# Gate weights as half sums over 512 columns, four gate blocks open, and branch products two to a bank

## The chip, the core and the metric

The kernel is one program on one core of one Trainium2 chip. The time is the device time of one execution in microseconds. Three executions of the kernel before took 3128.62, 3154.54 and 3169.11 us, median 3154.54. A further execution was recorded by the profiler; it took 3130.84 us, and every row below is from it.

## What is computed

Two layers of a diffusion backbone over 256 latent tokens (stream x) and 256 context tokens (stream xc), 1024 channels, float32. Each layer has a token mixer with four branches (window attention, differential attention, a convolution, a pooling mixer) and then a feed-forward part that looks up 16 of 16384 experts for each of 8 heads and each token. The changed code is in the merge of the four branches:

```python
def merge_branches(h, ys, w_gate, b_gate, w_branch, w_out):
    acc = jax.nn.sigmoid(h @ w_gate[0] + b_gate[0]) * (ys[0] @ w_branch[0])
    for n in range(1, N_BRANCH):
        acc = acc + jax.nn.sigmoid(h @ w_gate[n] + b_gate[n]) * (ys[n] @ w_branch[n])
    return acc @ w_out
```

Here `h` is 256x1024 (tokens x channels), each `w_gate[n]` 1024x1024, each `ys[n]` 256x512 and each `w_branch[n]` 512x1024. The sums over 1024 and 512 channels are sums of products of 128 channels each on TensorE (PE).

The expert lookup reads, for each token and each chosen expert, one row of 1024 numbers of a table `u` and one of a table `v` from the chip's memory by index (gathers): 6 tiles of 128 tokens, 128 experts for each token, a `u` and a `v` row each.

## The kernel before, in words

**Stages.** The program runs in this order. (1) The mixer of the first layer for the context tokens (to about 410 us); its products are computed with float32 split into two parts (class `Split`), three matmuls for one. (2) The mixer of the first layer for the latent tokens (to about 1060 us), with the gathers of the first context tile in the background. (3) Gathers almost alone (to about 1760 us). (4) The mixer of the second layer, with the last context tile's gathers in the background (to about 2270 us). (5) The rest of the second layer, whose gathers end the program.

**The merge.** A branch's 1024 output channels are 8 blocks of 128. `both` works on four blocks at a time, called a quad below: it loads 512 columns of the branch's weights (tile `w`, 1 MB), then twice 256 columns of the gate's weights for all 1024 channels (tile `w`, 1 MB each). For each block, `gate_mm` sums 8 products of the gate in a PSUM bank, ScalarE (ACT) takes a tanh of it (L844, into `th`), `branch_mm` sums 4 products of the branch in another bank, and VectorE (DVE) multiplies and adds both into `accT` (L851 to L854). Both sums come from the two banks of tag `mm`. There are 8 quads in stage 1, 8 in stage 2 and 4 in stage 4; `gates`, the gate part alone, runs for two more branches in stage 4, where the tanh values are kept.

**Weights.** All weight tiles `w` are loaded by one queue (SP's, L228 in `wtile`) into three places of 1 MB:

```python
    def wplace(kb, c):
        return sb.tile([128, 2048], F, tag="w", name="w", bufs=WB)[:, :kb * c].rearrange("p (k c) -> p k c", k=kb)
```

with `WB = 3`. A load can be issued when the tile that last had its place has been read for the last time. SP issues in program order. The search for experts (`route`) takes the same places for its weights `w_q`, and the output projection (`out_proj`) for `w_out`. In stage 1, a loaded tile is copied into two parts (L173 on ACT, L174 on DVE), which live in row buffers `u` and `v`; then `w` itself is free again.

**Background.** `tick` puts pieces of other work (attention, convolution, pooling) between products of the merge, `pump` puts in gathers (`u_slot`, `v_slot`): a POOL instruction that starts a gather (L1018), a DVE instruction for each `u` row (L1026), and for each `v` row a DVE instruction (L1043) or two matmuls (L1050). The order of the instructions on each engine is fixed when the program is built, by a list scheduler that follows this order as a priority; on the chip each engine works through its list in order.

**PSUM.** Eight banks: two `mm`, two `at` (attention scores), two `tr` (transposes and attention outputs), and two for the gathers' sums `va`. The scheduler orders accesses of two engines to a bank, even where they touch different halves of it.

Of the kernel before, what the change touches and what calls it, by code (L numbers as in the profile page):

```python
# [8 lines left out]
F = mybir.dt.float32  # L9
# [5 lines left out]
OP = mybir.AluOpType  # L15
# [33 lines left out]
def body(ctx: ExitStack, tc: tile.TileContext, x_d, cc_d, cols_d, rows_d, w_mod, w_in, w_gate,  # L49
# [8 lines left out]
    def mm_ps():  # L58
        return pp.tile([128, 512], F, tag="mm", name="mm", bufs=2)
# [10 lines left out]
    def t2():  # L70
        return sb.tile([128, 512], F, tag="t2", name="t2", bufs=4)

# [782 lines left out]

    def gates(hT, N, l, n, dst_of):
        for c in range(4):
            w = wtile(w_gate[l, n, :, c * 256:(c + 1) * 256], like=hT)
            for b in range(2):
                gate_mm(w, b, hT, N, l, n, c * 2 + b, dst_of(c * 2 + b))  # L860

# [5 lines left out]

    def both(hT, ys, N, l, order, accT, first):

        for c in range(2):  # L870
            for n in order:
                wb = wtile(w_branch[l, n, :, c * 512:(c + 1) * 512], 4, 512, ys[n])
                for c2 in range(2):
                    w = wtile(w_gate[l, n, :, c * 512 + c2 * 256:c * 512 + (c2 + 1) * 256], like=hT)
                    for b in range(2):
                        blk = c * 4 + c2 * 2 + b
                        th = sb.tile([128, T], F, tag="th", name="th", bufs=2)
                        gate_mm(w, b, hT, N, l, n, blk, th)
                        branch_mm(wb, c2 * 2 + b, ys[n], N, th, accT[:, blk, :], first and n == order[0])

# [371 lines left out]
    ysplit(3, hk(4), kv_half("k", 0))  # L1252
    both(hc, ys, T, 0, (3,), accT, True)
    flush()
# [3 lines left out]
    pieces(cv, 16 - CV)  # L1258
    both(hc, ys, T, 0, (0,), accT, False)
    ysplit(1, ysb(0), hk(1)[:, 0])  # L1260
    both(hc, ys, T, 0, (1,), accT, False)
    flush()
    ysplit(2, ysb(1), kv_half("k", 0))
    both(hc, ys, T, 0, (2,), accT, False)
    while mods:
# [51 lines left out]
    credit[1] = RATE0[1]  # L1317
    both(h, ys, T, 0, (3,), accT, True)
# [3 lines left out]
    both(h, ys, T, 0, (0,), accT, False)  # L1322
    TICKS[1] = T2[2]
    credit[1] = RATE0[3]
    both(h, ys, T, 0, (1,), accT, False)
    flush()
    credit[1] = RATE0[4]
    both(h, ys, T, 0, (2,), accT, False)
    out_proj(accT, (2, 3), 0)
# [24 lines left out]
    accT = hslot()  # L1354
    both(h, ys, T, 1, (3,), accT, True)
    flush()
# [6 lines left out]
    TICKS[1] = T3  # L1363
    both(h, ys, T, 1, (2,), accT, False)
    tha = [ysb(2 + i) for i in range(2)]
    thc = [m4() for i in range(2)]
    gates(h, T, 1, 0, lambda blk: tha[blk // 4][:, blk % 4, :])
    gates(h, T, 1, 1, lambda blk: thc[blk // 4][:, blk % 4, :])

# [154 lines left out]
```

## Time and profile before

| what | us |
|---|---|
| executions shown | 3128.62, 3154.54, 3169.11 |
| profiled execution | 3130.84 |
| its span | 3129.0 |
| busy in it: PE, DVE, POOL, ACT | 2336.2, 2330.6, 1744.7, 667.8 |

The busy times are sums over stages that have different limits, and no engine is busy for more than three quarters of the span. A stage has to be read by itself: who waits in it, and for what. The time from a weight load's issue to its landing stands in the view of DMA issues, the wait that it causes in the view of waits, and the release of its place on SP's own timeline.

### The profile page before, as it was taken

Reading aid. Unit: us, or ns where it says so; the run is one execution under the profiler, and the core shown is the slowest. Engines: PE = TensorE matmul, PEld = TensorE weight load, DVE = VectorE, ACT = ScalarE, POOL = GpSimd, SP = SyncE. Lnnn points to the kernel's source line nnn. Section 1 sums busy time; section 2 is a strip of 40 time slices with the busy share of each in tenths; the row PEclk is TensorE's granted clock in tenths of the full one; section 3 lists DMA queues with packets and bytes.
Section 4 is the critical chain, followed back from the end, with each engine's and each line's share of the span. In section 5 each row is a group of like instructions: output and inputs, shape, how many; then the busy total and the mean of one; then the engine's idle time right before and its main releaser. Section 6 shows DMA issues by size and latency. Waiting matters only on the chain.

```text
span 3129.0 us, 32834 instructions
## 1 busy us (share of the span) xinstructions
PE 2336.2 (75%) x10524; PEld 1561.6 (50%) x10524; DVE 2330.6 (74%) x5221; ACT 667.8 (21%) x1577; POOL 1744.7 (56%) x1542
## 2 busy tenths in 40 slices
PE   7999998879876776665555589769997875545555
PEld 5878887667765542222111267557686542211111
DVE  5956669768987899957677759876657995566776
ACT  3445421223111221111000201023331221110001
POOL 0000027554355687777777757666404677777776
PEclk9999999989998897787688899889998998977888
DMA  9948978887799899999999999899947889999998
GB/s 309 318 140 262 312 248 312 306 295 280 284 348 359 326 386 380 337 365 359 389 409 406 353 332 387 313 362 338 347 162 261 277 313 388 408 341 395 403 409 332
DMA packets 436779, 1036.53 MB, mean 331 GB/s; under 512 B 30464, under 2 KB 226560, under 8 KB 436608
## 3 DMA queue, kind: packets, MB, share of 16 engines
q0 software_dynamic: 221184, 805.40, 68.0%
q1 hardware_dynamic: 211984, 226.25, 21.7%
q10 hardware_dynamic: 3440, 2.78, 0.3%
q8 instruction: 84, 1.38, 0.2%
q14 instruction: 87, 0.71, 0.1%
HBM read 1032.22 MB, written 2.10 MB: 331 GB/s over the span
## 4 chain that ended last, share of the span: by engine, by line
PE 28%; DVE 20%; issue 18%; DMA 17%; POOL 16%; ACT 1%; SPq 0%; ACTq 0%; POOLq 0%; DVEq 0%
PE mm L215 12%; POOL v L1018 10%; POOL u L1018 6%; DMA v<-in_v_dram,idx 5%; DVE u L1026 5%; DMA w<-in_w_gate_dram 4%; DMA u<-in_u_dram,idx 3%; DVE m L774 3%; DVE dacc L1043 2%; PE mm L213 2%; PE mm L211 2%; DMA w<-in_w_in_dram 2%; PE mm L212 2%; PE at L473 2%; PE va L1050 2%
## 5 line engine op out<-in xcount | busy, mean ns | idle before, releaser
L1018 POOL DMA_INDIRECT u<-in_u_dram,idx x768 | 859.9, 1120 | 933.9 <-DVE m L804 428.9
L1050 PE MATMUL va<-v,dg 128*128 128x512 f32 x1436 | 843.4, 725 | 533.1 <-DMA v<-in_v_dram,idx 450.6
L1026 DVE SCALAR_TENSOR_TENSOR u<-u,h 128x1024 f32<-128x1024 f32 x768 | 934.2, 1221 | 295.1 <-DMA u<-in_u_dram,idx 293.5
L1018 POOL DMA_INDIRECT v<-in_v_dram,idx x768 | 884.2, 1151 | 432.6 <-issue 182.9
L1050 PEld LDWEIGHTS va<-v,dg 128*128 128x128 f32 x1436 | 295.9, 222 | 1023.6 <-issue 789.8
L215 PE MATMUL mm<-hT,w 128*128 128x256 f32 (+1 forms) x2176 | 509.7, 385 | 114.3 <-DMA w<-in_w_gate_dram 79.3
L1043 DVE SCALAR_TENSOR_TENSOR dacc<-v,wt,dacc 128x1024 f32<-128x1024 f32 x403 | 516.3, 1281 | 94.8 <-DMA v<-in_v_dram,idx 80.7
L215 PEld LDWEIGHTS mm<-hT,w 128*128 128x128 f32 x2176 | 406.6, 203 | 189.3 <-issue 74.9
L1048 ACT ACTIVATE dg<-ident,wt 128x128 f32<-128x128 f32 x359 | 141.4, 400 | 933.0 <-PE va L1050 859.0
L774 DVE SCALAR_TENSOR_TENSOR m<-m,cols,m 128x256 f32<-128x256 f32 x360 | 158.9, 478 | 0.1
L212 PE MATMUL mm<-hT,whi 128*128 128x256 f32 x512 | 143.9, 281 | 0.8 <-DVE hT L174 0.8
L211 PE MATMUL mm<-hT,whi 128*128 128x256 f32 x448 | 128.1, 286 | 4.0 <-ACT whi L173 3.2
L213 PE MATMUL mm<-hT,whi 128*128 128x256 f32 x448 | 127.2, 284 | 1.2 <-DVE whi L174 0.8
L215 PE MATMUL mm<-w,hT 128*128 128x256 f32 x512 | 118.5, 391 | 5.9 <-DMA w<-in_w_in_dram 5.9
L174 DVE TENSOR_TENSOR whi<-w,whi 128x1024 fp32r<-128x1024 f32 x86 | 104.1, 1221 | 16.4 <-ACT whi L173 8.9
L215 PEld LDWEIGHTS mm<-w,hT 128*128 128x128 f32 x512 | 100.0, 197 | 22.0 <-issue 7.8
L173 ACT CAST whi<-w 128x1024 fp32r<-128x1024 f32 x86 | 88.4, 1048 | 66.9 <-PE mm L213 49.9
L215 PE MATMUL mm<-ys,w 128*128 128x256 f32 x384 | 95.0, 385 | 6.3 <-ACT th L844 3.9
L212 PEld LDWEIGHTS mm<-hT,whi 128*128 128x128 f32 x512 | 97.3, 190 | 1.7 <-DVE hT L174 1.0
L844 ACT ACTIVATE th<-mm,cols 128x256 f32<-128x256 f32 x80 | 37.9, 474 | 268.8 <-PE mm L215 217.4
L211 PEld LDWEIGHTS mm<-hT,whi 128*128 128x128 f32 x448 | 85.5, 191 | 6.4 <-ACT whi L173 3.9
L213 PEld LDWEIGHTS mm<-hT,whi 128*128 128x128 f32 x448 | 85.0, 190 | 6.8 <-DVE whi L174 3.6
(339 smaller groups left out, 2831.7 us busy)
## 6 DMA issues: line engine op xcount, KB each, us to landing
w<-in_w_gate_dram SPq DMA_DIRECT2D x48, 1024.0 KB, 11.7
w<-in_w_in_dram SPq DMA_DIRECT2D x42, 1024.0 KB, 10.6
X<-in_w_mod_dram SPq DMA_DIRECT2D x40, 512.0 KB, 5.3
wm<-in_w_mod_dram SPq DMA_DIRECT2D x40, 512.0 KB, 5.3
w<-in_w_branch_dram SPq DMA_DIRECT2D x20, 1024.0 KB, 8.0
w<-in_w_q_dram SPq DMA_DIRECT2D x20, 1024.0 KB, 15.5
u<-in_u_dram,idx POOLq DMA_INDIRECT x768, 6.5
v<-in_v_dram,idx POOLq DMA_INDIRECT x768, 6.6
```

What stands on the lines that cost most here:

```text
L173: nc.scalar.copy(hi.bitcast(FR), v)
L174: nc.vector.tensor_tensor(lo.bitcast(FR), v, hi, op=OP.subtract)
L211: nc.tensor.matmul(ps, ah, bh, start=first, stop=False)
L212: nc.tensor.matmul(ps, ah, bl, start=False, stop=False)
L213: nc.tensor.matmul(ps, al, bh, start=False, stop=last)
L215: nc.tensor.matmul(ps, a[:, kb, ca], b[:, kb, cb], start=first, stop=last)
L774: nc.vector.scalar_tensor_tensor(acc[:, b, :], yb[:, b, k:k + T], cols[:, l, cw + k:cw + k + 1], acc[:, b, :], op0=OP.mult, op1=OP.add)
L1018: nc.gpsimd.indirect_dma_start(out=r, out_offset=None, in_=table, in_offset=bass.IndirectOffsetOnAxis(ap=self.idx[:, j:j + 1], axis=0))
L1026: nc.vector.scalar_tensor_tensor(r, r, 1.0, self.h2, op0=OP.mult, op1=OP.mult, accum_out=self.act[:, j % 16:j % 16 + 1])
L1043: nc.vector.scalar_tensor_tensor(self.dacc, v, w, self.dacc, op0=OP.mult, op1=OP.add)
L1048: nc.scalar.activation(dg, ident, AF.Copy, scale=w)
L1050: nc.tensor.matmul(self.va[:, half, :], dg, v[:, half * 512:(half + 1) * 512], start=j == self.pe[0], stop=j == self.pe[-1])
```

## The change

Loads, sums and the drain of the merge are cut differently; what is computed stays.

- The gate's weights of a quad are loaded as two halves of the sum: channels 0 to 511 and 512 to 1023, each for all 512 columns of the quad (1 MB each, rows of 2 KB where they were 1 KB). The branch's weights are loaded after them, not before.
- `gate_quad` adds the first half into four blocks, then the second half; the four sums are open at the same time, two to a bank of `mm`. A block's tanh follows its second half.
- After that the branch's products of the quad are made, two blocks to a bank of tag `tr`, and DVE takes two blocks (512 columns) in one instruction.
- The tanh values live in `t2`, which gets a fifth buffer; the tag `th` goes. `tick` and `pump` are called twice as often with half the amount.

```diff
-        return sb.tile([128, 512], F, tag="t2", name="t2", bufs=4)
+        return sb.tile([128, 512], F, tag="t2", name="t2", bufs=5)
...
-    def gate_mm(w, b, hT, N, l, n, blk, dst):
-        pg = mm_ps()
-        product(pg[:, :N], w, slice(b * 128, (b + 1) * 128), hT, slice(0, N))
-        tick(TICKS[1])
-        pump(3.5)
-        j = C_BG + n * 8 + blk
-        nc.scalar.activation(dst, pg[:, :N], AF.Tanh, scale=0.5, bias=cols[:, l, j:j + 1])
+    def half_product(ps, a, ca, b, cb, k0, first, last):
+        k = a.shape[1]
+        for kb in range(k):
+            f, z = first and kb == 0, last and kb == k - 1
...
+                nc.tensor.matmul(ps, a[:, kb, ca], b[:, k0 + kb, cb], start=f, stop=z, skip_group_check=True)
+
+    def gate_quad(hT, l, n, c, dsts):
+        ws = [wtile(w_gate[l, n, i * 512:(i + 1) * 512, c * 512:(c + 1) * 512], 4, 512, hT) for i in range(2)]
+        ps = [mm_ps() for i in range(2)]
+        for i in range(2):
+            for b in range(4):
+                half_product(ps[b // 2][:, b % 2 * T:(b % 2 + 1) * T], ws[i], slice(b * 128, (b + 1) * 128), hT,
+                             slice(0, T), 4 * i, i == 0 and b % 2 == 0, i == 1)
+                tick(TICKS[1] / 2)
+                pump(1.75)
+                if i == 1:
+                    j = C_BG + n * 8 + c * 4 + b
+                    nc.scalar.activation(dsts[b // 2][:, b % 2], ps[b // 2][:, b % 2 * T:(b % 2 + 1) * T], AF.Tanh, scale=0.5,
+                                         bias=cols[:, l, j:j + 1])
...
-    def both(hT, ys, N, l, order, accT, first):
+    def both(hT, ys, l, order, accT, first):
         for c in range(2):
             for n in order:
+                ths = [t2().rearrange("p (b t) -> p b t", b=2) for i in range(2)]
+                gate_quad(hT, l, n, c, ths)
                 wb = wtile(w_branch[l, n, :, c * 512:(c + 1) * 512], 4, 512, ys[n])
-                for c2 in range(2):
-                    w = wtile(w_gate[l, n, :, c * 512 + c2 * 256:c * 512 + (c2 + 1) * 256], like=hT)
+                for i, th in enumerate(ths):
+                    pb = tr_ps()
                     for b in range(2):
-                        blk = c * 4 + c2 * 2 + b
-                        th = sb.tile([128, T], F, tag="th", name="th", bufs=2)
-                        gate_mm(w, b, hT, N, l, n, blk, th)
-                        branch_mm(wb, c2 * 2 + b, ys[n], N, th, accT[:, blk, :], first and n == order[0])
+                        product(pb[:, b * T:(b + 1) * T], wb, slice((2 * i + b) * 128, (2 * i + b + 1) * 128), ys[n], slice(0, T))
+                        pump(1.8)
...
+                        nc.vector.scalar_tensor_tensor(th, th, 1.0, pb, op0=OP.add, op1=OP.mult)
+                        nc.vector.tensor_tensor(dst, dst, th, op=OP.add)
```

The order on PE at the end of stage 2, in the last two quads (branch 2, `ys2`, both halves of the columns). Before, `w_7785` and `w_7841` are the gate tiles of the first of the two quads and `w_7783` its branch tile, `w_7905`, `w_7961` and `w_7903` those of the second. In the scheduler's program the load of `w_7905` waits for the last matmul that reads `w_7841`, that of `w_7961` for the last that reads `w_7783`:

```order
L215 MATMUL mm_7844<-hT_4759,w_7841 128x256 x8
L215 MATMUL mm_7860<-ys2_5192,w_7783 128x256 x4
L215 MATMUL mm_7874<-hT_4759,w_7841 128x256 x8
L215 MATMUL mm_7890<-ys2_5192,w_7783 128x256 x4
L215 MATMUL mm_7908<-hT_4759,w_7905 128x256 x8
L215 MATMUL mm_7924<-ys2_5192,w_7903 128x256 x4
L215 MATMUL mm_7938<-hT_4759,w_7905 128x256 x8
L215 MATMUL mm_7954<-ys2_5192,w_7903 128x256 x4
L215 MATMUL mm_7964<-hT_4759,w_7961 128x256 x8
```

The change, same place. `w_7653` and `w_7655` are the two gate halves of the first quad, `w_7719` its branch tile; `w_7763`, `w_7765` and `w_7835` are those of the second. The load of `w_7763` waits for the last read of `w_7653`, that of `w_7765` for the last of `w_7655`, that of `w_7835` for the last of `w_7719`:

```order
L850 MATMUL mm_7658<-hT_4683,w_7653 128x256 x8
L850 MATMUL mm_7657<-hT_4683,w_7655 128x256 x4
L850 MATMUL mm_7658<-hT_4683,w_7655 128x256 x2
L850 MATMUL mm_7657<-hT_4683,w_7655 128x256 x4
L850 MATMUL mm_7658<-hT_4683,w_7655 128x256 x2
L215 MATMUL tr_7721<-ys2_5116,w_7719 128x256 x2
L850 MATMUL mm_7658<-hT_4683,w_7655 128x256 x4
L215 MATMUL tr_7721<-ys2_5116,w_7719 128x256 x6
L215 MATMUL tr_7744<-ys2_5116,w_7719 128x256 x8
L850 MATMUL mm_7767<-hT_4683,w_7763 128x256 x8
L850 MATMUL mm_7768<-hT_4683,w_7763 128x256 x8
L850 MATMUL mm_7767<-hT_4683,w_7765 128x256 x4
```

Gate and branch products alternated block by block; now 32 gate matmuls of a quad stand nearly together and 16 branch matmuls after them, and a quad's gate half comes free 16 matmuls before the quad's gate part ends.

The loads on SP's queue that belong to it, before:

```order
L228 DMA w_7686<-in_w_q_dram 128x8x256
L228 DMA w_7783<-in_w_branch_dram 128x4x512
L228 DMA w_7785<-in_w_gate_dram 128x8x256
L1077 DMA kt_8039<-in_kt_dram 128x256
L228 DMA w_7841<-in_w_gate_dram 128x8x256
L228 DMA w_7903<-in_w_branch_dram 128x4x512
L228 DMA w_7905<-in_w_gate_dram 128x8x256
L228 DMA w_7961<-in_w_gate_dram 128x8x256
```

and with the change:

```order
L228 DMA w_7529<-in_w_branch_dram 128x4x512
L228 DMA w_7556<-in_w_q_dram 128x8x256
L228 DMA w_7653<-in_w_gate_dram 128x4x512
L228 DMA w_7655<-in_w_gate_dram 128x4x512
L1104 DMA kt_7887<-in_kt_dram 128x256
L228 DMA w_7719<-in_w_branch_dram 128x4x512
L228 DMA w_7763<-in_w_gate_dram 128x4x512
L228 DMA w_7765<-in_w_gate_dram 128x4x512
L228 DMA w_7835<-in_w_branch_dram 128x4x512
```

The branch tile moved behind the two gate tiles of its quad; the number of loads is the same, and the `w_q` loads of the expert search stand among them as before.

## Rows read from the trace of the kernel before

**Rows 1.** The page: busy time of each engine, its share, instructions.
```profile
PE 2336.2 (75%) x10524; PEld 1561.6 (50%) x10524; DVE 2330.6 (74%) x5221; ACT 667.8 (21%) x1577; POOL 1744.7 (56%) x1542
```

**Rows 2.** Stretches: length; busy PE, PEld, DVE, ACT, POOL (count); clock; DMA share; GB/s.
```profile
146.00:410.00 264.00, 256.98 (x2119) 212.66 (x2117) 152.64 (x371) 120.71 (x248) 0.00 (x0) 1.00 0.74 243
...
450.00:1060.00 610.00, 501.88 (x2349) 406.19 (x2349) 502.77 (x1140) 134.58 (x312) 321.85 (x266) 0.91 0.87 313
...
560.00:900.00 340.00, 294.45 (x1373) 231.05 (x1371) 280.42 (x658) 92.45 (x219) 153.42 (x136) 0.93 0.82 294
...
2000.00:2270.00 270.00, 231.55 (x1079) 172.22 (x1079) 181.25 (x307) 75.62 (x191) 155.21 (x131) 0.94 0.93 344
...
2420.00:3129.00 709.00, 429.84 (x1012) 184.72 (x1010) 511.48 (x1056) 95.38 (x233) 511.08 (x484) 0.86 0.95 363
```

**Rows 3.** Who waited for gate loads issued in 560 to 900 us: us, times.
```profile
  PE mm L215: 49.6, 8
  PEld mm L215: 18.5, 3
```

**Rows 4.** Waits in 2000 to 2270 us: us in total, times, longest.
```profile
PE mm L215 <- DMA w<-in_w_gate_dram: 29.6, 3, 10.9
PEld mm L215 <- DMA w<-in_w_gate_dram: 22.1, 2, 11.1
```

**Rows 5.** DMA issues: 560 to 900 (three rows), 100 to 410 (two), 1990 to 2150.
```profile
w<-in_w_gate_dram SPq DMA_DIRECT2D x15, 1024.0 KB, 12.0
w<-in_w_branch_dram SPq DMA_DIRECT2D x7, 1024.0 KB, 7.3
w<-in_w_q_dram SPq DMA_DIRECT2D x4, 1024.0 KB, 12.5
...
w<-in_w_gate_dram SPq DMA_DIRECT2D x16, 1024.0 KB, 7.8
w<-in_w_branch_dram SPq DMA_DIRECT2D x8, 1024.0 KB, 7.8
...
w<-in_w_gate_dram SPq DMA_DIRECT2D x9, 1024.0 KB, 16.7
```

**Rows 6.** PE's timeline, 884 to 925 us and 604 to 606: start, us, [idle before].
```profile
884.27 3.62 PE L215 MATMUL mm<-hT,w 128*128 128x256 f32 x16
887.72 1.89 PE L215 MATMUL mm<-ys,w 128*128 128x256 f32 x8
...
914.11 5.73 PE L215 MATMUL mm<-hT,w 128*128 128x256 f32 x16 [14.14 <-DMA w<-in_w_gate_dram]
...
604.12 1.12 PE L473 MATMUL at<-ka,q 64*128 64x512 f32 x2
605.17 1.10 PE L499 MATMUL tr<-va__359,t 128*128 128x64 f32 x8
606.17 0.61 PE L495 MATMUL tr<-ident,t 128*128 128x128 f32 x4
```

**Rows 7.** SP's timeline, 560 to 960 us: start, us.
```profile
898.28 2.09 SPq L228 DMA_DIRECT2D w<-in_w_gate_dram  x2
```

**Rows 8.** Line L844 (the tanh): who waited for it (us, times).
```profile
  PEld mm L215: 8.3, 9
  PE mm L215: 4.5, 8
```

**Rows 9.** Groups by line and shape: busy us, mean ns.
```profile
L844 ACT ACTIVATE th<-mm,cols 128x256 f32<-128x256 f32 x80 | 37.9, 474 | 268.8 <-PE mm L215 217.4 <-PE mm L213 46.6 <-DVE m L774 4.7
L854 DVE TENSOR_TENSOR hT<-hT,th 128x256 f32<-128x256 f32 x56 | 23.4, 418 | 0.6
L1065 DVE TENSOR_TENSOR X<-X,dacc 128x512 f32<-128x512 f32 x24 | 15.6, 686 | 0.0
L1026 DVE SCALAR_TENSOR_TENSOR u<-u,h 128x1024 f32<-128x1024 f32 x768 | 934.2, 1221 | 295.1 <-DMA u<-in_u_dram,idx 293.5 <-DVE m L853 0.8
```

**Rows 10.** The chain of waits, 560 to 930 us: a convolution piece on DVE.
```profile
824.81 4.75 DVE m L774 x12
```

More of the change, by code (lines that the diff above doesn't have):

```diff
@@ L834, in pool @@
             yield
-    def gate_mm(w, b, hT, N, l, n, blk, dst):
-        pg = mm_ps()
-        product(pg[:, :N], w, slice(b * 128, (b + 1) * 128), hT, slice(0, N))
-        tick(TICKS[1])
-        pump(3.5)
-        j = C_BG + n * 8 + blk
-        nc.scalar.activation(dst, pg[:, :N], AF.Tanh, scale=0.5, bias=cols[:, l, j:j + 1])
+    def half_product(ps, a, ca, b, cb, k0, first, last):
+        k = a.shape[1]
+        for kb in range(k):
+            f, z = first and kb == 0, last and kb == k - 1
+            if isinstance(a, Split):
+                (ah, al), (bh, bl) = a.at(kb, ca), b.at(k0 + kb, cb)
+                nc.tensor.matmul(ps, ah, bh, start=f, stop=False, skip_group_check=True)
+                nc.tensor.matmul(ps, ah, bl, start=False, stop=False, skip_group_check=True)
+                nc.tensor.matmul(ps, al, bh, start=False, stop=z, skip_group_check=True)
+            else:
+                nc.tensor.matmul(ps, a[:, kb, ca], b[:, k0 + kb, cb], start=f, stop=z, skip_group_check=True)
[12 more added lines that the diff above has]
+                                         bias=cols[:, l, j:j + 1])
     def branch_mm(wb, bl, y, N, th, dst, first):
@@ L854, in branch_mm, with gates @@
             nc.vector.tensor_tensor(dst, dst, th, op=OP.add)
[L856 to L860, printed above, removed]
+    def gates(hT, l, n, dsts):
+        for c in range(2):
+            gate_quad(hT, l, n, c, [dsts[c][:, 2 * i:2 * i + 2] for i in range(2)])
     def branches(y, N, th_of, accT, ws):
@@ L866, in branches @@
                 tick(TICKS[2])
-    def both(hT, ys, N, l, order, accT, first):
+    def both(hT, ys, l, order, accT, first):
         for c in range(2):
             for n in order:
+                ths = [t2().rearrange("p (b t) -> p b t", b=2) for i in range(2)]
+                gate_quad(hT, l, n, c, ths)
                 wb = wtile(w_branch[l, n, :, c * 512:(c + 1) * 512], 4, 512, ys[n])
-                for c2 in range(2):
-                    w = wtile(w_gate[l, n, :, c * 512 + c2 * 256:c * 512 + (c2 + 1) * 256], like=hT)
+                for i, th in enumerate(ths):
+                    pb = tr_ps()
                     for b in range(2):
-                        blk = c * 4 + c2 * 2 + b
-                        th = sb.tile([128, T], F, tag="th", name="th", bufs=2)
-                        gate_mm(w, b, hT, N, l, n, blk, th)
-                        branch_mm(wb, c2 * 2 + b, ys[n], N, th, accT[:, blk, :], first and n == order[0])
+                        product(pb[:, b * T:(b + 1) * T], wb, slice((2 * i + b) * 128, (2 * i + b + 1) * 128), ys[n], slice(0, T))
+                        pump(1.8)
+                    pb = pb.rearrange("p (b t) -> p b t", b=2)
+                    dst = accT[:, c * 4 + 2 * i:c * 4 + 2 * i + 2, :]
+                    if first and n == order[0]:
+                        nc.vector.scalar_tensor_tensor(dst, th, 1.0, pb, op0=OP.add, op1=OP.mult)
+                    else:
+                        nc.vector.scalar_tensor_tensor(th, th, 1.0, pb, op0=OP.add, op1=OP.mult)
+                        nc.vector.tensor_tensor(dst, dst, th, op=OP.add)
     def out_proj(accT, tiles, l, ws=None):
@@ L1252, in body @@
     ysplit(3, hk(4), kv_half("k", 0))
-    both(hc, ys, T, 0, (3,), accT, True)
+    both(hc, ys, 0, (3,), accT, True)
     flush()
@@ L1258, in body @@
     pieces(cv, 16 - CV)
-    both(hc, ys, T, 0, (0,), accT, False)
+    both(hc, ys, 0, (0,), accT, False)
     ysplit(1, ysb(0), hk(1)[:, 0])
-    both(hc, ys, T, 0, (1,), accT, False)
+    both(hc, ys, 0, (1,), accT, False)
     flush()
     ysplit(2, ysb(1), kv_half("k", 0))
-    both(hc, ys, T, 0, (2,), accT, False)
+    both(hc, ys, 0, (2,), accT, False)
     while mods:
@@ L1317, in body @@
     credit[1] = RATE0[1]
-    both(h, ys, T, 0, (3,), accT, True)
+    both(h, ys, 0, (3,), accT, True)
     before([(diff_attn(qc, 0, 0, n, part(ys[1], n), False), 5) for n in range(2)])
@@ L1321, in body @@
     credit[1] = RATE0[2]
-    both(h, ys, T, 0, (0,), accT, False)
+    both(h, ys, 0, (0,), accT, False)
     TICKS[1] = T2[2]
     credit[1] = RATE0[3]
-    both(h, ys, T, 0, (1,), accT, False)
+    both(h, ys, 0, (1,), accT, False)
     flush()
     credit[1] = RATE0[4]
-    both(h, ys, T, 0, (2,), accT, False)
+    both(h, ys, 0, (2,), accT, False)
     out_proj(accT, (2, 3), 0)
@@ L1354, in body @@
     accT = hslot()
-    both(h, ys, T, 1, (3,), accT, True)
+    both(h, ys, 1, (3,), accT, True)
     flush()
@@ L1363, in body @@
     TICKS[1] = T3
-    both(h, ys, T, 1, (2,), accT, False)
+    both(h, ys, 1, (2,), accT, False)
     tha = [ysb(2 + i) for i in range(2)]
     thc = [m4() for i in range(2)]
-    gates(h, T, 1, 0, lambda blk: tha[blk // 4][:, blk % 4, :])
-    gates(h, T, 1, 1, lambda blk: thc[blk // 4][:, blk % 4, :])
+    gates(h, 1, 0, tha)
+    gates(h, 1, 1, thc)
     flush()
```

## The prediction, as it was made before the changed kernel ran

> **What bounds the kernel now.** I read the busy times first. No engine is busy for more than 75% of the span [rows 1], so the bound has to be looked for stage by stage, and the change touches only the merge: 8 quads inside 146 to 410 us, 8 inside 560 to 930 us, 4 quads and two gate-only branches inside 2000 to 2270 us.
>
> The view of stretches comes next. In the first of them PE is busy for 257.0 of 264.0 us [rows 2]: it is bound by PE's work, and there is nothing to wait less for. In 560 to 900 us PE is idle for 340.0 - 294.5 = 45.5 us while DVE and the DMA engines have only 82% each; in 2000 to 2270 us PE is idle for 38.5 us with the DMA engines at 93% [rows 2]. So in these two no resource is full.
>
> The view of waits says what PE lacks there. Gate loads issued in 560 to 900 us held PE up for 49.6 + 18.5 = 68.1 us in 11 waits, counting its weight loads too [rows 3], and those in 2000 to 2270 us for 29.6 + 22.1 = 51.7 us in 5 [rows 4]. The timelines show why. A gate load of the second stretch lands after 12.0 us in the middle [rows 5], and it is issued too late: at 898.28 us [rows 7], with only one branch block left to compute, and PE stands still for 14.14 us until 914.11 [rows 6].
>
> **How late a load is, from the order.** I call lead the PE work that stands between the matmul that frees a load's place and the first matmul that reads the load. From the start of one gate block to the next group PE takes 3.45 us for 8 matmuls, 0.43 us each [rows 6]; attention's matmuls take 0.56 us (scores), 0.28 us (outputs) and 0.15 us (transposes) each [rows 6]. Added up between the two places in the order before, the leads of the 16 gate loads in 560 to 930 us are 8.4, 13.9, 6.1, 9.8, 6.1, 12.9, 5.0, 15.9, 2.2, 10.9, 2.0, 10.6, 4.7, 10.7, 1.7 and 10.4 us. What each lacks to 12.0 us sums to 67.4 us, against 68.1 us measured, so the method may be trusted. In the order of the change they are 15.9, 17.3, 20.7, 11.8, 18.7, 12.5, 13.4, 16.9, 7.9, 15.4, 13.9, 15.2, 8.8, 16.8, 13.9 and 13.0 us: a place comes free halfway through the gate part, and 16 to 32 matmuls follow before the next load is needed. They lack 7.5 us in all. The branch loads have leads of 11.3 us or more against a landing of 7.3 us [rows 5], so they cost nothing. The five `w_q` loads stand among them on the same queue and are moved too: their leads go from 7.5, 9.1, 12.3, 10.4, 5.2 to 5.6, 5.4, 14.3, 7.4, 8.7 us, which at 12.5 us [rows 5] is 18.0 us of lack before and 22.9 after.
>
> **The change part by part.**
>
> *Latent quads of the first layer.* -67.4 + 7.5 + 22.9 - 18.0 = -55 us of lack. PE's idle time of all kinds is 45.5 us plus the 14.1 us at 914 us, 59.6 us, so of 68.1 us of waits 0.875 show as idle PE: -48 us. Ends: -59.6 (all of it) and -12 (the second rival below).
>
> *Quads of the second layer.* Here landing takes 16.7 us [rows 5]. Leads before: 12.5, 14.0, 2.6, 15.5, 3.5, 16.8, 5.0, 16.7 us, lacking 47.1 (51.7 measured). With the change: 21.7, 16.5, 5.5, 8.2, 12.1, 10.6, 14.8, 19.5, and for the first two gate-only loads 10.6 and 17.0, lacking 38.6 us; at 14.7 us of landing 26.5. That is -9 or -21; I take -14, with 0 and -27 as ends.
>
> *The clock.* After the wait at 914 us the first 16 records take 5.73 us where they take 3.62 with PE running [rows 6], 2.1 us more; the granted clock of the two stretches is 0.93 and 0.94 [rows 2]. 16 waits could give 34 us; some ten go, but shorter ones stay. I take half of ten, -10 us.
>
> *Wider rows of the loads* (2 KB for 1 KB). In 100 to 410 us, without gathers, gate loads of 1 KB rows and branch loads of 2 KB rows both land after 7.8 us [rows 5]: 0. The other end is the 7.3 against 12.0 us in the second stretch [rows 5], but there two gate loads are often issued together; it would bring the last lacks to nothing, -7 us.
>
> *Two blocks to a bank, tanh.* PE now has to wait with a second block's last matmuls until ACT has read the first block of the bank; 48 such places (24 groups of four, two banks each). Nearest rows: the tanh takes 474 ns [rows 9], and where PE waited for one it cost 8.3 + 4.5 = 12.8 us in 17 waits, 0.75 us each [rows 8]. Four matmuls of the other bank, 1.7 us, mostly stand between. Ends 0 and 48 x 0.75 = 36 us; I take a third of 0.75 us in the 32 places outside the first stage, +8 us.
>
> The Trainium skill, PSUM — Partial Sum Buffer, section "Summary: rules for kernel authors", speaks against this part: who reads PSUM while a matmul runs should have a different bank. By it every one of the 48 is a full wait, the +36 us end; the rows leave that open, since before no two blocks shared a bank.
>
> *Branch products in the transposes' banks, DVE.* DVE's 418 ns per 256 columns become 686 ns per 512 [rows 9], some 10 us less in all, on an engine that is not at its limit: 0. That transposes must share their two banks with sums that DVE has to drain is a rival below. The halved ticks and pumps keep their sum: 0. In the context stage PE sets the time and its matmuls stay: 0, at most 7 us either way.
>
> *Sum.* -48 - 14 - 10 + 8 = -64 us of PE's time. Not all of it reaches the end: gathers run behind the merge in the same program order and must speed up as well. The DMA engines' work in 450 to 1060 us is 0.87 x 610 = 531 us; at the 0.95 that they reach over the last 709 us [rows 2] it takes 559 us, so at most 51 us can go there, and in 2000 to 2270 us 0.93 x 270 / 0.95 = 264, 6 us. I take three quarters, **-48 us**. The profiled execution took 3130.8 us, 24 us below the median of the runs shown, 3154.5; against its own time the sum gives 3083, against the median 3106.5. I forecast the median: **3107 us**.
>
> **The rivals.**
>
> *Transfers take it back* (3142 us). Loads that are issued earlier run beside more gathers, and landing in the second stretch rises to the 16.7 us of the third [rows 5]. The leads then lack 42.0 + 22.9 us against 67.4 + 18.0 before, -20 x 0.875 = -18, nothing in the second layer, -2 of clock, +8 of tanh: -12. For it: DMA share of 0.93 where landing is slow. Against: 0.82 where most of the gain is.
>
> *All of it arrives* (3082 us). The tanh waits are covered, and DMA and DVE follow: -48 - 14 - 10 = -72. It needs a DMA share of about 0.97 in 450 to 1060 us, above any row of that length.
>
> *The shared bank* (3128 us). All 48 tanh waits are full: -72 + 36 = -36, three quarters -27. For it: ACT's list holds attention's copies as well, so a tanh may come late. Against: 1.7 us of other matmuls in front.
>
> *Slower: branch sums hold the transposes' banks* (3178 us). DVE takes its list in order. If a drain of a pair of blocks stands behind `u` rows (1.22 us each [rows 9]) or a convolution piece (4.75 us [rows 10]), attention's transposes, and PE behind them, wait for the bank. There are 24 pairs in the two latent stages; from 2.0 us each it eats the 48 us. At 3.0 us, between the ends, 24 x 3.0 - 48 = +24; at 4.75 us +66. Against: a gate half of 7 us without transposes mostly follows on PE.
>
> *That the change does not do what it says* is excluded by the order: places do come free earlier.
>
> **How the numbers follow.** Chances: forecast 0.42 (its own range 3080 to 3130), transfers 0.20, all 0.20, shared bank 0.10, slower 0.08. The range 3055 to 3165 reaches past the third rival by the half spread of the runs shown and past the second by the same; it leaves out the slower rival and the outer end of the third. 2% is about what a measurement of this kernel tells from no change: below 3091 us lie most of "all of it arrives" and a quarter of the forecast, 0.27; above 3218 only the outer end of the slower rival, 0.03; the rest is 0.70.
>
> **What the profile of the changed kernel would show.** Right: PE's waits for gate loads fall to a quarter in 560 to 930 us and to about two thirds in 2000 to 2270; short waits for `w_q` appear; the DMA share of the second stretch rises above 0.88; the stage ends some 35 to 50 us earlier; the context stage keeps its length. Wrong: landing times of 16 us or more in the second stretch with gate waits still above 30 us; PE waiting for the tanh for over 20 us; PE's transposes waiting for DVE's drains, or gathers waiting for DVE with the stage as long as before.

## The result, and the profile after

The change made the kernel slightly slower. In 20 executions each, before took 3138.98 us in the median and the changed kernel 3148.29; the ratio is 1.0075, 95% interval 1.0053 to 1.0098. Timed again later it was 1.0038 (1.0007 to 1.0070). I had forecast 48 us of gain. The profiled execution took 3139.65 us, before 3130.84.

The page after, its line of busy times and of weight loads (which answers to [rows 1]):

```profile
PE 2374.0 (76%) x10524; PEld 1592.3 (51%) x10524; DVE 2327.5 (74%) x5153; ACT 666.5 (21%) x1577; POOL 1761.9 (56%) x1542
```

PE runs the same 10524 matmul records and is busy 37.8 us longer. Where, the view of stretches tells. I cut both programs at the same events: the first gather, the issue of the first `w_out` load behind the latent merge, the first and the last gather of the fourth of the six token tiles, and the end. Rows are, in turn, the context stage from 146 us, the latent stage up to the end of its merge ("latent merge" below), expert search and gathers, the second layer's mixer, the rest. Columns: stretch, length; busy PE, PEld, DVE, ACT, POOL with counts; granted clock; DMA share; GB/s. Before:

```profile
146.00:430.00 284.00, 271.31 (x2204) 225.31 (x2203) 165.94 (x436) 129.77 (x274) 0.00 (x0) 0.99 0.71 232
430.00:925.00 495.00, 426.25 (x1992) 345.02 (x1991) 411.94 (x935) 111.85 (x259) 258.23 (x213) 0.93 0.85 304
925.00:1758.00 833.00, 534.24 (x1397) 265.15 (x1395) 654.95 (x1490) 120.66 (x293) 623.70 (x555) 0.82 0.98 373
1758.00:2255.00 497.00, 409.90 (x1799) 311.70 (x1800) 370.06 (x664) 101.04 (x250) 315.21 (x256) 0.91 0.93 343
2255.00:3129.00 874.00, 569.12 (x2024) 312.27 (x2022) 619.82 (x1424) 142.92 (x408) 547.01 (x513) 0.87 0.89 335
```

After:

```profile
146.00:437.00 291.00, 273.26 (x2210) 231.63 (x2209) 161.14 (x410) 128.73 (x274) 0.08 (x1) 0.97 0.68 227
437.00:954.00 517.00, 448.10 (x1984) 359.01 (x1983) 423.38 (x925) 113.53 (x261) 272.18 (x223) 0.88 0.82 296
954.00:1783.00 829.00, 527.68 (x1404) 267.79 (x1403) 646.04 (x1471) 118.93 (x291) 608.39 (x547) 0.83 0.98 372
1783.00:2255.00 472.00, 410.99 (x1790) 311.73 (x1789) 369.29 (x650) 99.63 (x247) 320.93 (x255) 0.92 0.96 358
2255.00:3138.00 883.00, 590.30 (x2032) 320.38 (x2031) 619.74 (x1424) 144.04 (x409) 559.81 (x514) 0.84 0.89 334
```

The second layer's mixer gained 25 us, the latent merge lost 22 and the context stage 7. In the latent merge PE is idle for 517 - 448.1 = 68.9 us, before for 495 - 426.25 = 68.75, and does the same work in 22 us more at a clock of 0.88 instead of 0.93. So the stage was given a gain, and lost more than it had been given.

The gain is there. The view of DMA issues of the change, 560 to 900 us ([rows 5] before):

```profile
w<-in_w_gate_dram SPq DMA_DIRECT2D x12, 1024.0 KB, 9.2
w<-in_w_branch_dram SPq DMA_DIRECT2D x6, 1024.0 KB, 6.1
w<-in_w_q_dram SPq DMA_DIRECT2D x4, 1024.0 KB, 15.1
```

Its waits in the latent merge, 437 to 954 us, and the wait for gate loads in 2000 to 2270 us (us, times, longest; [rows 3, 4] before):

```profile
PE mm L215 <- DMA w<-in_w_q_dram: 28.6, 4, 11.4
PE tr L495 <- ACT t L518: 7.9, 5, 2.9
...
PE at L473 <- ACT t L639: 4.1, 1, 4.1
PE tr L505 <- DVE ys L673: 4.0, 1, 4.0
PE mm L850 <- DMA w<-in_w_gate_dram: 3.2, 1, 3.2
```
```profile
PE mm L850 <- DMA w<-in_w_gate_dram: 8.2, 4, 6.1
```

PE waits 3.2 us for gate loads in the latent merge, where it had waited 49.6. In place of that it waits 28.6 us for `w_q` and some 20 us for attention's own chain.

Where the clock went is seen on PE's timeline after, 590 to 633 us (start, us, [idle before]); L850 is the gate, L473 to L499 are window attention:

```profile
590.61 7.13 PE L850 MATMUL mm<-hT,w 128*128 128x256 f32 x32
600.63 0.66 PE L495 MATMUL tr<-ident,t 128*128 128x128 f32 x4 [2.89 <-ACT t L518]
601.22 1.12 PE L473 MATMUL at<-ka,q 64*128 64x512 f32 x2
602.27 1.66 PE L499 MATMUL tr<-va__359,t 128*128 128x64 f32 x8
603.72 0.31 PE L477 MATMUL at<-mask,identb 128*128 128x128 bf16 x1
603.83 1.06 PE L495 MATMUL tr<-ident,t 128*128 128x128 f32 x4
604.82 2.07 PE L473 MATMUL at<-ka,q 64*128 64x512 f32 x2
...
629.09 3.73 PE L850 MATMUL mm<-hT,w 128*128 128x256 f32 x8
```

and in the view of stretches, that time and a second such run:

```profile
603.00:633.00 30.00, 29.12 (x91) 18.78 (x91) 15.64 (x27) 10.90 (x26) 13.54 (x12) 0.50 0.71 248
695.00:722.00 27.00, 25.02 (x76) 15.88 (x75) 15.52 (x27) 7.30 (x21) 15.54 (x16) 0.50 0.79 268
```

After a wait of 2.89 us the clock fell to its lower level, 1.2 GHz. PE was then busy for 29.12 of 30 us, until 629.09 us with units of attention and not one gate or branch matmul among them, and the clock stayed there; the scores took 2.07 us instead of 1.12 [rows 6]. It rose again, at 633 us, behind the gate's matmuls. The second profile of the changed kernel has both runs at the same places (604 to 635 and 696 to 727 us), so this is no chance of one execution. The Trainium skill, TensorE: Matmul & The Clock Gate, section "Why this matters for your kernels", tells kernels to keep TensorE busy and free of idle gaps between bursts of matmuls. The trace agrees on the fall, after an idle gap of 2.89 us; that being busy again is enough to come back to the full level is not borne out by this row (29.12 of 30 us at 0.50), and the measurement decides.

Why attention stands there alone, the order shows. Gate blocks 0 and 1 share a bank. Block 1's second half waits for ACT, that is for the tanh of block 0, and stands behind six units of attention:

```
2724 L850 MATMUL mm_5735<-hT_4683,w_5733 128x256 [waits DMAHW0_49]
2725 L850 MATMUL mm_5735<-hT_4683,w_5733 128x256 x3
2726 L850 MATMUL mm_5736<-hT_4683,w_5733 128x256 x4
2727 L495 MATMUL tr_5751<-ident_73,t2_5749 128x128 [waits Activation_49]
...
2767 L850 MATMUL mm_5735<-hT_4683,w_5733 128x256 [waits Activation_49]
```

On ACT, 598 to 634 us, that tanh (L865) runs at 625.97 us, 28 us after the last gate matmul in front of the run had ended (590.61 + 7.13 = 597.7 us):

```profile
599.80 0.69 ACT L518 ACTIVATE t<-at,ast 128x512 f32<-128x512 f32 x1 [4.34 <-DVE idx L985]
...
625.97 0.48 ACT L865 ACTIVATE t<-mm,cols 128x256 f32<-128x256 f32 x1
```

Its output is a `t2` tile. The five places of `t2` serve attention too (`e` and `eT`, two tiles for each unit), and a place goes to whichever instruction is scheduled first: in the program this tanh's tile has the place that two of attention's tiles had just before it, though it was created ahead of them. And since the gate half stays in use until after the run, its place comes free late. SP's timeline (start, us; two gate loads are one row): the second of them could not be issued until 47 us after the first and held the queue for that time, and `w_q` stood behind it:

```profile
594.32 47.73 SPq L228 DMA_DIRECT2D w<-in_w_gate_dram  x2
649.46 0.37 SPq L228 DMA_DIRECT2D w<-in_w_q_dram  x1
```

### The profile page after: what moved, and what is told of

Its sections match the earlier page's. It is cut to its first block, busy times and chain, and to the rows that moved or that the text cites. A ratio compares the mean times of both kernels' runs of the same rounds, so it can differ in the third digit from the quotient of the medians.

```text
span 3137.9 us, 32649 instructions
## 1 busy us (share of the span) xinstructions
PE 2374.0 (76%) x10524; PEld 1592.3 (51%) x10524; DVE 2327.5 (74%) x5153; ACT 666.5 (21%) x1577; POOL 1761.9 (56%) x1542
## 4 chain that ended last, share of the span: by engine, by line
PE 31%; DVE 18%; issue 18%; POOL 16%; DMA 16%; ACT 2%; POOLq 0%; SPq 0%; ACTq 0%; DVEq 0%
POOL v L1045 10%; PE mm L215 7%; POOL u L1045 6%; DVE u L1053 5%; DMA v<-in_v_dram,idx 5%; PE mm L850 4%; DMA u<-in_u_dram,idx 4%; DMA w<-in_w_q_dram 3%; PE va L1077 3%; DVE dacc L1070 2%; PE tr L215 2%; DVE m L774 2%; PE at L473 2%; DMA w<-in_w_in_dram 2%; PE tr L499 1%
## 5 line engine op out<-in xcount | busy, mean ns | idle before, releaser
L1077 PE MATMUL va<-v,dg 128*128 128x512 f32 x1436 | 857.3, 738 | 507.4 <-DMA v<-in_v_dram,idx 427.2
L1045 POOL DMA_INDIRECT v<-in_v_dram,idx x768 | 896.5, 1167 | 429.6 <-issue 188.2
L1077 PEld LDWEIGHTS va<-v,dg 128*128 128x128 f32 x1436 | 307.7, 231 | 1001.5 <-issue 817.8
L215 PE MATMUL mm<-hT,w 128*128 128x256 f32 (+1 forms) x1152 | 247.9, 372 | 63.5 <-DMA w<-in_w_q_dram 37.2
L850 PE MATMUL mm<-hT,w 128*128 128x256 f32 x1024 | 256.9, 398 | 18.2 <-DMA w<-in_w_gate_dram 11.5
L850 PEld LDWEIGHTS mm<-hT,w 128*128 128x128 f32 x1024 | 195.1, 199 | 53.6 <-issue 22.5
L215 PE MATMUL tr<-ys,w 128*128 128x256 f32 x384 | 85.6, 379 | 1.7 <-DMA w<-in_w_branch_dram 1.7
L215 PE MATMUL mm<-hT,wk 128*128 128x256 f32 (+1 forms) x416 | 80.5, 349 | 2.4 <-ACT sc L1120 1.5
L215 PEld LDWEIGHTS tr<-ys,w 128*128 128x128 f32 x384 | 72.3, 190 | 11.9 <-issue 2.5
L846 PE MATMUL mm<-hT,whi 128*128 128x256 f32 x256 | 76.8, 301 | 0.1
L215 PEld LDWEIGHTS mm<-hT,wk 128*128 128x128 f32 x416 | 68.5, 190 | 13.3 <-issue 2.4
L212 PE MATMUL mm<-hT,whi 128*128 128x256 f32 x256 | 72.8, 285 | 0.9 <-DVE hT L174 0.9
```

The costliest lines, as they stand in the source:

```text
L212: nc.tensor.matmul(ps, ah, bl, start=False, stop=False)
L215: nc.tensor.matmul(ps, a[:, kb, ca], b[:, kb, cb], start=first, stop=last)
L846: nc.tensor.matmul(ps, ah, bh, start=f, stop=False, skip_group_check=True)
L850: nc.tensor.matmul(ps, a[:, kb, ca], b[:, k0 + kb, cb], start=f, stop=z, skip_group_check=True)
L1045: nc.gpsimd.indirect_dma_start(out=r, out_offset=None, in_=table, in_offset=bass.IndirectOffsetOnAxis(ap=self.idx[:, j:j + 1], axis=0))
L1077: nc.tensor.matmul(self.va[:, half, :], dg, v[:, half * 512:(half + 1) * 512], start=j == self.pe[0], stop=j == self.pe[-1])
```

## The experiments

The theory at first: the new order puts attention in long runs on PE, and the clock and the late loads eat the gain. Its rivals: the stage lengths of one profile are scatter; tanh pairs in attention's places hold attention up; sums in the transposes' banks do; waits for `w_q` do, and the clock follows. "PE's busy time at the low clock" in the expectations is the time of PE's records that start while the granted clock is 0.5, overlaps counted once: 99 us in the latent merge after, 41 before.

The kernel before took 3212, 3136 and 3209 us in the median in the three sessions in which these ran (1 to 4; 5 to 8; 9 to 11); ratios are to before in the same session. Merge, PE idle in it, clock and the second layer's mixer are from one profile each:

| kernel | ratio (95%) | latent merge us | PE idle | clock | 2nd mixer us |
|---|---|---|---|---|---|
| before; again | | 495; 504 | 69; 75 | 0.93; 0.93 | 497; 499 |
| change; again | 1.0075; 1.0038 | 517; 519 | 69; 69 | 0.88; 0.88 | 472; 470 |
| 1 second layer only | 0.9954 (0.9922 to 0.9986) | 497 | 74 | 0.94 | 470 |
| 2 own tanh places | 0.9927 (0.9897 to 0.9956) | 492 | 66 | 0.92 | 473 |
| 3 and spread | 0.9942 (0.9912 to 0.9972) | 463 | 51 | 0.95 | 488 |
| 4 and scores' banks | 0.9862 (0.9811 to 0.9912) | 452 | 33 | 0.96 | 494 |
| 7 wide matmuls between | 0.9984 (0.9944 to 1.0024) | 500 | 59 | 0.92 | 471 |
| 8 spread in latent only | 0.9798 (0.9745 to 0.9851) | 435 | 26 | 0.98 | 471 |
| 9 pairs only | 1.0165 (1.0124 to 1.0206) | 541 | 99 | 0.88 | 490 |
| 10 as 8, scores' banks in 2nd | 0.9848 (0.9815 to 0.9881) | 448 | 31 | 0.97 | 478 |
| 11 as 8, gate's banks in 2nd | 0.9853 (0.9818 to 0.9889) | 452 | 33 | 0.96 | 467 |

**1. The change in the second layer alone.**

```diff
-    both(h, ys, 0, (3,), accT, True)
+    both_old(h, ys, T, 0, (3,), accT, True)
... (all eight calls of the first layer; both_old is before's merge)
```

> The new merge runs in the second layer alone; the context and latent stages of the first layer have the merge of before. Theory (runs of attention): in the first layer the new order puts attention's small matmuls on PE in two long runs, 14.9 and 12.4 us of work, without gate or branch matmuls between; the clock goes to 0.5 in them, 99 us of PE's busy time in the latent merge at the low clock against 41 before, and the gain from the gate loads is eaten there; in the second layer the gain stays (497 us before, 473 after). So here: latent merge 490 to 500 us, second layer's mixer 470 to 480, in all 20 to 30 us faster than before, ratio 0.990 to 0.994. Rival (the stage lengths of one profile each are scatter, and the change costs a little everywhere): ratio 1.000 to 1.005.

The stages came as expected, 497 and 470 us, and the ratio just above the range: the change is worth its gain in the second layer. That the stage lengths are scatter of a single profile is out, also by the repeated profiles (5 and 6).

**5 and 6. Both kernels again**, unchanged.

> The changed kernel again, on the same chip as the runs beside it: a second profile of its stages. If the first profile's stages are typical, the latent merge takes 505 to 530 us here as well with 85 us or more of PE's busy time at the low clock, the second layer's mixer 465 to 480, and the ratio to before is 1.004 to 1.011. If they were scatter of one profile, the latent merge is within 490 to 503.

> The kernel before again: a second profile of its stages. Expected if one profile is typical: latent merge 490 to 500 us, second layer's mixer 490 to 503, context stage ended at 428 to 433 us.

Merge 519 against 504 us, mixer 470 against 499; the changed kernel's ratio 1.0038 was just below its range, and before's merge just above its own. Two profiles of one kernel agree in these stages to 9 us. The second one of before took 3161.9 us, 26 us over the median of its session, so its stages are long rather than typical, and the 15 us between the merges rather too few.

**2. Places of their own for the tanh pairs.**

```diff
-        return sb.tile([128, 512], F, tag="t2", name="t2", bufs=5)
+        return sb.tile([128, 512], F, tag="t2", name="t2", bufs=3)
-                ths = [t2().rearrange("p (b t) -> p b t", b=2) for i in range(2)]
+                ths = [sb.tile([128, 512], F, tag="th", name="th", bufs=2).rearrange("p (b t) -> p b t", b=2) for i in range(2)]
```

> The change with the tanh pairs in two places of their own, three places left for attention's tiles. In the order the runs of attention on PE get longer: 18.7, 11.5 and 8.0 us of work. Theory (runs of attention): latent merge 515 to 540 us, over 90 us of PE's busy time in it at the low clock; ratio to before 1.004 to 1.012. Rival (the tanh pairs, which sit in attention's places until their branch sums are drained, hold attention up): with places of their own the latent merge falls below 505 us, ratio under 1.002.

My theory, as put there, failed: the merge fell to 492 us. ACT's timeline of this kernel, 590 to 598 us; the stretch of the first run of attention, and that of a second run; and PE's wait for `w_q` in the merge:

```profile
593.14 0.47 ACT L865 ACTIVATE th<-mm,cols 128x256 f32<-128x256 f32 x1 [0.58 <-PE mm L850]
```
```profile
598.00:628.00 30.00, 29.07 (x155) 19.48 (x154) 25.54 (x45) 15.38 (x38) 19.16 (x17) 0.97 0.93 338
678.00:697.00 19.00, 16.74 (x95) 10.93 (x94) 14.38 (x28) 7.97 (x21) 13.54 (x13) 1.00 0.92 315
```
```profile
PE mm L215 <- DMA w<-in_w_q_dram: 28.0, 4, 11.3
```

The tanh follows its sum by 0.58 us. The same 30 us now hold 155 matmul records instead of 91, at 0.97 instead of 0.50. I had counted runs allowing a few gate matmuls within one; here groups of 4 to 10 gate records stand among the units, in the change none. SP held its two gate loads for 7.28 us instead of 47.73. So the rival was right: late tanh tiles made that run. Nor does a run bring the clock down by its length: from 679 to 697 us PE has units of attention alone here too, with no wait above 0.93 us among them, and the clock stays at 1.00. What costs in these traces is a wait ahead of such a run: the clock falls, and the run does not bring it back. PE's waits for `w_q` are what they were with the change (28.6 us), so the place that came free late was not their cause.

**3. Attention's pieces over all twelve groups of a quad.** Before, a quad's pieces were put in after each of four gate blocks, with a branch block in between; the change puts them all in the gate part and none in the branch part.

```diff
-                tick(TICKS[1] / 2)
+                tick(TICKS[1] / 3)
...
                         product(pb[:, b * T:(b + 1) * T], wb, ...
+                        tick(TICKS[1] / 3)
                         pump(1.8)
```

> As the kernel with the tanh pairs in places of their own, and the calls that put in pieces of attention are spread over all twelve groups of four matmuls of a quad (eight of the gate, four of the branch, a third of the amount each) and no longer over the gate's eight alone. In the order no run of attention is over 7.1 us of work. Theory (runs of attention): PE's busy time at the low clock in the latent merge falls under 65 us, the merge takes 475 to 497 us, ratio to before 0.988 to 0.996, at least 15 us less than without the spreading. Rival (branch sums and attention share the transposes' two banks): the sharing is the same here, so the merge stays above 510 us, ratio 1.003 or more. Second rival (waits for w_q behind the gate loads on the queue): two of the w_q loads now have leads of 29 and 32 us, two gate loads only 3; the waits change places, merge 500 to 515, ratio 0.998 to 1.003.

The merge fell by 29 us to 463, lower than expected. The ratio lies in the range that I gave, but it is no better than that of kernel 2: the second layer's mixer went from 473 to 488 us, and the rest of the program behind it was 20 us longer (931 against 911 us in the two profiles), which I do not explain. In the second layer the spreading does harm (its two gate-only branches, moreover, get only two thirds of the pieces); kernels 4 and 10, 494 and 478 us with the same banks, agree.

**4. Branch sums in the scores' banks.**

```diff
-                    pb = tr_ps()
+                    pb = at_ps()
```

> As the spread kernel, and the branch sums go to the two banks of attention's scores instead of those of the transposes. In the order no run of attention is over 5.6 us. Theory (runs of attention): about as the spread kernel or up to 10 us faster, low-clock time under 60 us, ratio 0.984 to 0.994. Rival (the transposes' banks): only this one gains, by 15 us or more on the spread kernel with branch sums in the transposes' banks.

11 us less in the merge, PE idle 33 instead of 51 us: sharing the transposes' banks costs less than the rival said. That it costs anything is likely but not shown, since one order's merge differs by 17 us between profiles (8, 10 and 11). The rest of the step in the ratio lies in stages that are the same in both, and I do not explain it.

**7. The clock by itself.**

```diff
         pt = tr_ps()
+        if wide_mm:
+            nc.tensor.matmul(pt, ident, X[:, 2, :512], start=True, stop=True)
```

> The changed kernel with one more matmul in each of the 16 units of window attention of the latent stage: 128 columns by 512, into the bank that the unit's transposes then overwrite. It computes nothing that is used, and costs 16 x 0.87 = 14 us of PE's time at full speed; the two runs of attention stay where they are. Theory (a wait of some 3 us ahead of a run of attention lets the clock fall, and attention's small matmuls do not bring it back, wide ones do): PE's busy time at the low clock in the latent merge falls from 99 to under 70 us and the merge is as long as the changed kernel's or shorter in spite of the 14 us, 500 to 518 us; ratio to before 1.000 to 1.008. Rival (the waits alone make the stage long, the clock is a by-product): the merge grows by 10 to 16 us, ratio 1.010 to 1.016. Third case (attention runs low whatever stands between): low-clock time grows, merge 535 or more.

PE's timeline and the stretch of the first run (L497 is the added matmul):

```profile
605.29 2.02 PE L497 MATMUL tr<-X,ident 128*128 128x512 f32 x2
607.11 1.06 PE L499 MATMUL tr<-ident,t 128*128 128x128 f32 x4
...
608.20 1.12 PE L473 MATMUL at<-ka,q 64*128 64x512 f32 x2
...
610.20 1.08 PE L497 MATMUL tr<-X,ident 128*128 128x512 f32 x2
```
```profile
606.00:636.00 30.00, 29.68 (x140) 18.15 (x139) 26.59 (x46) 14.73 (x35) 22.66 (x18) 0.96 0.90 306
690.00:720.00 30.00, 26.27 (x101) 16.11 (x102) 24.14 (x47) 9.78 (x25) 20.54 (x17) 0.77 0.81 270
```

The first added matmul still takes 2.02 us, the next 1.08: the clock was back at 2.4 GHz. With 14 us of useless work the merge is 19 us shorter than the changed kernel's in the same session (500 and 519), and low-clock time fell from 101 to 51 us. The low clock is a cause, not a by-product. The ratio, 0.9984, is a little better than the range of the theory. The second run was not cured altogether: it still has a clock of 0.77.

**8. The repaired change.** Own places everywhere; in the latent stage alone, pieces spread and sums in the scores' banks (`f=3, bank=at_ps`; elsewhere `f=2, bank=tr_ps`).

```diff
-    both(h, ys, 0, (3,), accT, True)
+    both(h, ys, 0, (3,), accT, True, 3, at_ps)
... (the four calls of the latent stage)
```

> The change with own places for the tanh pairs everywhere; in the latent stage attention's pieces spread over all twelve groups and branch sums in the banks of the scores; the context stage and the second layer with the amounts and banks of the change. Theory: latent merge 448 to 465 us as in the spread kernel with the scores' banks, second layer's mixer 465 to 478 instead of 494, so 15 to 25 us below that kernel; ratio to before 0.976 to 0.985. Rival (time gained in the merge is given back in the gathers behind it, which the second layer's mixer only seemed to lose): ratio 0.984 to 0.990, with the mixer at 485 or more.

Both stages came as expected or better. This kernel beats the kernel before by 2.0% (1.5 to 2.6), and the changed kernel, 3150.5 us in the same session, with 3073.4 us. Its stretches (latent merge, search and gathers, mixer) and waits in the merge:

```profile
433.00:868.00 435.00, 409.22 (x1983) 333.79 (x1982) 397.35 (x892) 111.40 (x258) 259.75 (x204) 0.98 0.90 328
868.00:1725.00 857.00, 547.90 (x1407) 278.29 (x1406) 666.88 (x1504) 121.08 (x294) 642.59 (x565) 0.79 0.99 372
1725.00:2196.00 471.00, 405.99 (x1791) 309.17 (x1790) 369.74 (x651) 99.03 (x247) 316.68 (x255) 0.92 0.96 360
```
```profile
PE mm L215 <- DMA w<-in_w_q_dram: 9.2, 2, 6.6
PE mm L850 <- DMA w<-in_w_gate_dram: 7.0, 3, 3.8
```

**9. The pairs without the halves.** Before's gate loads and sums, but two branch blocks to a bank and tanh pairs in `t2`.

```diff
-                        th = sb.tile([128, T], F, tag="th", name="th", bufs=2)
-                        gate_mm(w, b, hT, N, l, n, blk, th)
-                        branch_mm(...)
+                        gate_mm(w, b, hT, N, l, n, c * 4 + c2 * 2 + b, th[:, b])     (th: a pair from t2)
+                    pb = tr_ps()     (then two products and one drain, as in the change)
```

> The kernel before, with the branch products two blocks to a bank of the transposes and one drain for two blocks (tanh pairs in attention's places, five of them), but the gate's weights loaded as before, 256 columns at a time, one block's sum after the other. By the lead method the gate loads of the latent merge lack some 53 us to a landing of 12.0 us (67 before, 7.5 with the change), those of w_q more than before. Theory (the halves bring the leads, the pairs bring nothing): PE's waits for gate loads in the latent merge stay at 35 to 60 us, the merge at 490 to 515 us, ratio 0.996 to 1.006. Rival (fewer, wider drains and free sum banks are what gains): merge under 480, ratio under 0.992.

Worse than expected, 1.0165: the pairs alone, with the tanh pairs in attention's places, cost some 53 us (0.0165 x 3209), with 99 us of idle PE in the merge and the clock at 0.88. PE's waits in the merge, 456 to 997 us:

```profile
PE mm L215 <- DMA w<-in_w_gate_dram: 41.8, 5, 11.7
PE mm L215 <- DMA w<-in_w_q_dram: 19.9, 4, 10.9
PE tr L495 <- ACT t L518: 15.4, 3, 10.0
```

The waits for gate loads stay, as the theory said (49.6 us before, 3.2 with the change), and 15.4 us of waits for attention's exponentials are new. So the halves bring the gain, and the drain by pairs, as the change places it and its tanh tiles, brings the loss.

**10 and 11. Other banks in the second layer.**

> As the kernel that spreads attention in the latent stage only, and the second layer's branch sums too go to the banks of the scores. The second layer's gate loads then have leads of 20.2, 15.0, 11.7, 14.7, 17.1, 17.7, 8.7, 13.9, 6.3 and 18.8 us, 32 us short of a landing of 16.7 where they were 38 short. Theory: second layer's mixer 462 to 475 us, ratio 0.976 to 0.984, not told apart from the kernel with the transposes' banks (0.9798). Rival (scores wait for drains): mixer above 480, ratio above 0.985.

> The same with the second layer's branch sums in the gate sums' own two banks, so that a new quad's gate sums start only when DVE has drained the branch sums. Leads there: 21.7, 16.5, 15.1, 19.7, 17.5, 16.7, 25.3, 23.5, 20.9 and 19.5 us, 2 us short of 16.7 in all. Theory by leads alone: PE's waits for gate loads fall to under 10 us there and the mixer to 445 to 460, ratio 0.970 to 0.978. Rival (DMA engines at 0.93 to 0.97 of their time in that stretch set its end, and the drains make new waits): mixer 465 to 480, ratio 0.978 to 0.986.

Neither is told apart from 8: the mixers of 478 and 467 us lie about its 471. The 478 is 3 us above the range of the theory; in 11 the rival's mixer came, not that of the leads. In 11 no wait for a gate load is left there, as the leads said (9.3 us in the mixer of 8), yet the mixer is hardly shorter: PE waits 21.0 us for `v` rows in it, in 8 17.5. The merge of these two, 448 and 452 us in the same order as the 435 of 8, shows how far one profile scatters.

## Why the prediction was wrong

Two terms of the sum failed, the halved ticks that I put at 0 and the tanh that I put at +8 for a wait of another kind. Curing both (2 and 3) took 54 to 56 us off a latent merge that was to be 48 us shorter and was 15 to 22 us longer.

- *Gate loads, -55 us of lack*: right in kind. PE's waits for them went from 49.6 to 3.2 us, and with what follows mended the merge shrank by 45 us (497 to 452, kernels 1 and 4 of one session), against my -48. The check of the method was wrong, though: 68.1 us counts three waits twice. The 18.5 us of PE's weight loads (PEld) end with PE's own waits for the same loads, at 636.42, 701.8 and 757.5 us, so 49.6 us were measured, and 29.6 in the second layer, not 51.7. The first of them on both timelines:

```profile
636.42 0.50 PEld L215 LDWEIGHTS mm<-hT,w 128*128 128x128 f32 x2 [7.45 <-DMA w<-in_w_gate_dram]
636.42 1.22 PE L215 MATMUL mm<-hT,w 128*128 128x256 f32 x2 [6.62 <-DMA w<-in_w_gate_dram]
```

  The price of the scores was off too: 0.56 us is one of two records of a scores matmul, a whole one takes 1.05 us (604.12 to 605.17 us in [rows 6]). In all, the lacks of 67.4 us exceed the measured waits by a third. That -48 came out near the 46 us which those waits lost is in part luck: the factor of 0.875 took back some of the double count.
- *Halved ticks and pumps, 0*: **the first step that failed.** They "keep their sum", but before, the ticks were spread over gate and branch and now they fall into the gate part alone. Spreading them again (3, on top of 2) gave 29 us of the latent merge.
- *Two blocks to a bank, tanh, +8*: **the second step that failed**, wrong in kind. I priced ACT's 474 ns and the wait of PE for it. The tanh's new place among attention's tiles I did not price: it made the tanh 28 us late, and the shared bank then kept gate matmuls and the half's place behind it. Own places gave 25 to 27 us (517 and 519 to 492). The PSUM page's rule on reading a bank while a matmul runs, in the Trainium skill (PSUM — Partial Sum Buffer, "Summary: rules for kernel authors"), pointed at the right bank; the price that I worked out by it, a full wait each, +36, is not what was paid, for no wait of PE for a tanh stands among its waits in the latent merge: the scheduler had moved the matmuls behind it.
- *Clock, -10*: wrong sign. I counted only the waits that go. Weighing PE's records at the low clock against the same forms at full clock, the merge lost 48 us to it after and 20 before: +28. A wait in front of gate matmuls cost some 2 us of clock (5.73 us for 3.62 [rows 6]); one in front of a run of attention was followed by 30 us at half speed, some 15 us lost.
- *`w_q`, +5*: too small. In the merge PE's waits for it rose from 1.9 to 28.6 us. The leads are counted in PE's work; before, PE's own waits for gate loads gave these loads more time, and that cover went with them: so I argue, no run separates it. The late place (47.73 us) is not the cause, for without it (2) the waits were 28.0 us; with the pieces spread and the scores' banks they fell to 9.2 (8).
- *Transposes' banks* (the slower rival): at most small. The one pair of profiles says 11 us of merge, within the 17 us by which one order's merge scatters.
- *Second layer, -14*: right in kind, -25 to -29 measured; PE's waits for gate loads fell from 29.6 to 8.2 us, further than the leads said.
- *Context stage, 0 at most 7*: it took 7 and 9 us more. With own tanh places (2 to 4, 8, 10, 11) it took 1 to 6 us more than the 284 of before, so part may lie with those places; no run isolates it.
- *Three quarters arrive*: fair. In 8 the merge is 60 to 69 us shorter and the mixer 26 to 28, and search and gathers take 18 to 24 us longer than before; of 86 to 97 us, 63 arrived (0.0202 x 3136).

The signs I had named: gate waits fell, as said; the DMA share of 560 to 900 us fell to 0.79 instead of rising above 0.88, and the stage ended 29 us later, which is what showed the forecast wrong.

The account of the latent merge: 517 to 519 us as changed, 492 with own tanh places, 463 with the pieces spread, 452 (435 to 452) with the scores' banks; 495 to 504 before.

## What to carry to other kernels

When a change frees an engine from one wait, reread who shares the places of each new tile and between which instructions background work falls: a tile that moves into another chain's buffers inherits that chain's pace. Where PE works off small matmuls by itself, put some wide ones among them; a short wait in front of such a run cost more clock here (some 15 us lost behind 2.89 us of wait) than a wait of 14 us in front of wide ones (2 us). A sum of waits for loads is not a gain until the loads queued behind them have been given their own leads.

## What the runs showed of the hardware that I had not expected

PE can be busy for 29.12 of 30 us and be granted 0.50 throughout, and the same kind of work, right behind gate matmuls, went on at 1.00 (679 to 697 us of kernel 2); one matmul of 128x512 per unit of attention, 0.9 to 1.1 us of extra work each, brought the same stretch to 0.96. In one session the kernel before took 3136 us in the median, in two others 3209 and 3212, so that only ratios within a session can be compared. In which stages the difference lies is not shown: the profiles of the same merge order at hand, 3161.9 and 3174.7 us long (504 and 497 us of merge, 839 and 859 us of search and gathers), are 13 us apart and not 73.
